# A two-layer hybrid decoder on one core: the last quarter of the first down projection by token with seven block products, and the query projection in another order

## The chip, the cores and the metric

The kernel runs on 1 core of one Trainium2 chip. The metric is the device time of one execution in microseconds. Before the change it is 2163.66 us, the median of 3 runs (2163.54 to 2163.85).

## The reference

One sequence of 256 tokens with 2048 features (float32) goes through two residual layers, each a token mixer and then a ConvFFN, and a last RMSNorm. Only these parts bear on the change:

```python
def rmsnorm(x, g):
    r = lax.rsqrt(jnp.mean(xf * xf, axis=-1, keepdims=True) + EPS)
    return (xf * r).astype(x.dtype) * g

def conv_ffn(xn, w_up, conv_w, conv_b, w_down):
    h = xn @ w_up                                  # 2048 -> 2 * 5632
    ...                                            # causal depthwise conv of width 3
    return (jax.nn.silu(gate) * val) @ w_down      # 5632 -> 2048

def reference(...):
    ...
    h = h + conv_ffn(rmsnorm(h, f_norm[0]), ...)            # first layer's FFN
    k_sh, v_sh, c_sh = fox_shared_kv(h, kv_norm, ...)       # reads rmsnorm(h, kv_norm)
    ...
    q, g = split(rmsnorm(h, b_norm[0]) @ w_qg)              # second layer: queries and gates
    q = rmsnorm(q.reshape(B, S, N_HEADS, HEAD_DIM), q_norm)
    ...
```

So the place in question is the seam between the layers: the first FFN's down projection (5632 to 2048 features) is added to the residual `h`, and the next matrix product, the queries (2048 to 2048 features), needs all 2048 features of the new `h`.

## The kernel before

**Precision.** Each float32 product is made of three TensorE (PE) products of rounded parts: every operand is split into a rounded part (`hi`) and the remainder (`lo`), and hi·hi, hi·lo and lo·hi are summed in PSUM. ScalarE (ACT) makes `hi` by a copy, VectorE (DVE) makes `lo` by a subtraction.

**The weight stream.** All weights come in chunks of 128 x 1024 floats (512 KB), one after the other, in one list (`Stream`). For each item of the list the loop in `run` issues, in this order, the load of the item 6 places on (a DMA in SP's queue into a tile `raw`), the split of the item 3 places on (ACT writes `whi`, DVE writes `wlo`), the matrix products of the item itself on PE, and then one step of every background generator (`advance`). A generator's `yield` therefore means: one chunk later. All engines run their own instructions in this written order. There are 4 buffers each of `raw`, `whi` and `wlo`, so the split of one chunk must wait until PE has done the chunk four places before it:

```python
if 0 <= i + LOADS < n:
    self._load(i + LOADS)
if 0 <= i + AHEAD < n:
    self._split(i + AHEAD)
...
    mult(*self.parts.pop(i))
    self.advance()
```

**Two forms of product.** By features (`feat_block`): the weights are the stationary operand, the result has features on partitions like `h`. By token (`tok_blocks`): the activations are stationary, the weights move, and the result has tokens on partitions, 512 output features a block, 8 chunks a block for 2048 input features. A whole chunk is 24 products of 256 columns in either form. After `between()` the next products are made with 512 columns each, 8 in the first chunk and 2 in the second (`state["wide"]`).

**Seven block products.** In the down projections a chunk by token can be taken as a 2 x 2 block product with seven block multiplications in place of eight (`seven_block`, `seven`): 21 products of 256 columns in place of 24, in two list items of 9 and 12. For that, sums of activation blocks are kept in the operand tile `X1`, which the up projection no longer needs, and sums of the weight blocks are made by DVE for each such chunk (`weight_sums`). A block's seven-product chunks leave sums in a second PSUM tile `m`, which are put together with the plain sums in a tile `Y` at the end of the block (`sums_apart`). `order_of` gives the order of plain and seven-product chunks in a block of 22.

**The seam before the change.** The first down projection has three blocks of 512 columns by token (2, 9 and 9 seven-product chunks). Their results have tokens on partitions and are turned by a DVE transpose of 32 x 32 blocks and a round trip through DRAM (`rows_out`, `rows_in`), then added to `h` (`rows_added`). The last 512 columns are two blocks by features (p = 6 and 7, 11 chunks each), whose results are added to `h` directly; while they run, `residual_prepared` makes the operand `X1` of the queries from the first 12 of 16 feature tiles of `h`. `residual` for p = 6 and 7 makes the last four, and starts the norm: `token_sums` sums the squares over the features with two small products on PE, makes the factor `rcol` of each token, and `token_rows` writes it to DRAM and reads it back as a row (`way_rb`, `rB`), on POOL's queue, for the gates later.

The query projection is four blocks by token, 8 chunks each, one block after the other. When a block is done, `head_norm` normalises its four heads in four steps: squares on ACT and two sums on DVE; twelve small DVE instructions for a reciprocal square root; and twice a scaling and a transpose on DVE, followed by a round trip through DRAM on SP's queue. Beside it `kv_operand` makes the operand `X2` of keys and values from `h`, one tile a step at most.

PSUM holds three tiles `ps` of two banks (`main_ps`) and two tiles `mp` of one bank (`misc_ps`).

Of the kernel before, what the change touches and what calls it, by code (L numbers as in the profile page):

```python
# [17 lines left out]
P = 128  # L18
# [115 lines left out]

class Phase:
# [28 lines left out]
def order_of(blk, lead=3):  # L164


    some, head, foot = {0: (SUMMED[:2], 18, 1), 3: (SUMMED[:6], lead, 5)}.get(blk, (SUMMED, lead, 0))
    plain, seven = [c for c in range(KF // 2) if c not in some], list(some)
    out, rest = [(c, False) for c in plain[:head]], [(c, False) for c in plain[len(plain) - foot:]]
    plain = plain[head:len(plain) - foot]  # L170
    n, m = len(plain), len(seven)
    for i, c in enumerate(plain):
        while len(seven) * n > (n - i - 1) * m and seven:
            out.append((seven.pop(0), True))
        out.append((c, False))
    return out + rest


def build(ctx, tc, d, out):
# [86 lines left out]
    def tok_blocks(blocks, x, K=KD, load=None, prep=None, place=None):  # L266
# [8 lines left out]
        for c, j0, nj in cuts:  # L275
            if prep and c == 3:
                s.then(at_mult=between)
            for i, ((src, done), box) in enumerate(zip(blocks, boxes)):
                def mult(hi, lo, c=c, j0=j0, nj=nj, done=done, box=box):
# [241 lines left out]
    def seven_block(blk, src, order, done, sums_done):  # L521
# [14 lines left out]
        def new_ps():  # L536
            if blk < 3:
                ps = main_ps()
                return lambda tb, w, n=T: ps[:, tb, w:w + n]
# [3 lines left out]
        def products(hi, lo, c, i, j, tb, cols=(0, T), left=0):  # L543
            for lower, part in ((0, hi), (0, lo), (1, hi)):
                n, left = 512 if left > 0 else 256, left - 1
                for w in cols[::n // 256]:
                    mm(box["ps"](tb, w, n), x()[:, 2 * c + j, lower * T + tb * P:lower * T + (tb + 1) * P],
                       part[:, j * 512 + w:j * 512 + w + n],
                       i == 0 and j == 0 and (w == 0 or blk == 3 and tb == 1) and part is hi and not lower,
# [3 lines left out]
        def plain(c, i):  # L553
            def mult(hi, lo):
                if i == 0:
                    box["ps"] = new_ps()
                if blk == 3 and i == 13:
                    s.start(three_blocks())
                if blk < 3 or i <= last - HELD:
# [69 lines left out]
    def sums_apart(blk):  # L629
# [4 lines left out]
        def sums(m):  # L634
            Y = ph.temp("apart", [P, 4, T], bufs=1)
# [7 lines left out]

        def done(ps):
            while "Y" not in box:
# [12 lines left out]
    def rows_added(blk, tb, way, place):  # L658
        for _ in range(3):
# [3 lines left out]
        for _ in range(5):  # L663
# [5 lines left out]
    def residual_prepared():  # L669

        for p in range(6):
            while state["added"] < 2 * (p // 2 + 1):
                yield
            for kt in (2 * p, 2 * p + 1):
                prep(X1, kt, C_BNORM)
                yield
# [8 lines left out]
        state["prepared"] = True  # L685
# [290 lines left out]
    def kv_operand():  # L976
        assert state["prepared"]
        att("X2")
        nc.vector.tensor_tensor(att("gain"), column(C_QNORM), column(C_KNORM), op=OP.mult)
        for _ in range(3):  # L980
            yield
        for kt in range(KD):
            prep(att("X2"), kt, C_KVNORM)
            for _ in range(1 + kt % 2):
                yield
# [40 lines left out]
    def head_norm(key, blk):  # L1026

        def done(*parts):
            parts = [(p, 4 // len(parts) * i) for i, p in enumerate(parts)]
# [211 lines left out]
    def g_done(p):  # L1241
        def done(ps, both):
# [4 lines left out]
            while state["done"] < 2 * p + 2 or state["gates"] < p:  # L1247
# [10 lines left out]
             "prepared": False, "wide": [8, 2]}  # L1258
# [51 lines left out]
    for blk in range(4):  # L1310
        seven_block(blk, d["down1"][22 * blk:22 * blk + 22], order_of(blk), final(blk) if blk < 3 else closing,
                    sums_into_residual(blk))
# [71 lines left out]
```

## Time and profile before

| | |
|---|---|
| Median of 3 runs | 2163.66 us |
| The profiled execution | 2163.74 us, its span 2162.0 us, granted PE clock 0.999 |
| Busy in the span | PE 2152.6, DVE 1649.4, ACT 1212.8, POOL 25.9 us |
| Third down block (by token, seven products) | 869.50 to 926.20 us |
| Two blocks by features | 926.28 to 986.23 us |
| Four query blocks | 986.23 to 1074.01 us |

Times in the rows are from the start of the span. PE is the matrix engine, PEld its weight loads, DVE VectorE, ACT ScalarE, POOL GpSimd, SP the engine that issues most DMAs; SPq is its queue. In a timeline row stand the start, the duration, the engine and line, the operation, `written<-read` tiles and the shape; in square brackets how long the engine had been idle before it, and what ended that. In the profile lines of the kernel before, line 216 is every matrix product, lines 112 and 113 the split of a plain chunk, 313 and 314 an operand tile from `h` (`X` or `att_X`, the program's `X1` and `X2`), 345 and 348 the factor's way through DRAM, 1037 to 1048 `head_norm`.

### The profile page before, as it was taken

What the parts mean: (1) busy time and instruction counts of PE and PEld (TensorE: products, weight loads), DVE (VectorE), ACT (ScalarE), POOL (GpSimd) and SP (SyncE); (2) the same over time, 40 slices, a digit from 0 to 9 for tenths busy, and PEclk for the clock granted to TensorE, in tenths of its full rate; (3) what the DMA queues carried; (4) which work ended last, traced back from release to release, by engine and by line L of the source; (5) the groups of instructions that cost most, each with busy time, mean ns of one, the idle gap of its engine ahead of it and who ended that gap; (6) DMA issues with size and microseconds to landing.
All of it is one profiled execution on the core that took longest, in us unless ns stands there. A gap on an engine that the chain in (4) does not pass through costs nothing.

```text
span 2162.0 us, 45349 instructions
## 1 busy us (share of the span) xinstructions
PE 2152.6 (100%) x18572; PEld 2136.3 (99%) x18572; DVE 1649.4 (76%) x2410; ACT 1212.8 (56%) x1692; POOL 25.9 (1%) x46
## 2 busy tenths in 40 slices
PE   9999999999999999999999999999999999999998
PEld 9999999999999999999999999999999999999998
DVE  6696687776777699976778886668777777779997
ACT  6665555555555555554545775445555555555555
POOL 0000000000000000000000200000000000000000
PEclk9999999999999999999999999999999999999999
DMA  8686566665666567776878877566866666666665
GB/s 311 189 241 205 193 199 194 190 200 184 203 192 194 176 200 228 225 226 179 266 249 260 255 230 234 186 221 197 267 194 195 193 196 192 194 191 188 204 204 166
DMA packets 159857, 454.68 MB, mean 210 GB/s; under 512 B 26320, under 2 KB 48608, under 8 KB 159264
## 3 DMA queue, kind: packets, MB, share of 16 engines
q1 hardware_dynamic: 158112, 447.82, 66.4%
q0 software_dynamic: 1072, 3.41, 0.7%
q8 instruction: 145, 2.38, 0.4%
q10 hardware_dynamic: 464, 0.55, 0.1%
q14 instruction: 64, 0.52, 0.1%
HBM read 434.39 MB, written 17.32 MB: 209 GB/s over the span
## 4 chain that ended last, share of the span: by engine, by line
PE 99%; DVE 0%; ACT 0%; issue 0%; POOL 0%; DVEq 0%; ACTq 0%; POOLq 0%
PE ps L216 98%; PE mp L216 1%; PE mp L780 0%; PE mp L1228 0%; PE ps L1225 0%; ACT sq L441 0%; DVE h_h L747 0%; DVE h_h L440 0%; DVE h_h L741 0%; PE mp L412 0%; ACT fin_t L733 0%; DVE fin_t L737 0%; DVE h_h L717 0%; DVE fin_y L736 0%; DVE rcol L738 0%
## 5 line engine op out<-in xcount | busy, mean ns | idle before, releaser
L113 DVE TENSOR_TENSOR wlo<-raw,whi 128x1024 fp32r<-128x1024 f32 (+1 forms) x732 | 887.3, 1218 | 270.5 <-ACT whi L112 266.3
L112 ACT ACTIVATE whi<-raw 128x1024 fp32r<-128x1024 f32 (+1 forms) x732 | 770.0, 1057 | 570.0 <-PE ps L216 448.5
L216 PE MATMUL ps<-X,whi 128*128 128x256 f32 (+1 forms) x6466 | 823.6, 280 | 0.0
L216 PEld LDWEIGHTS ps<-X,whi 128*128 128x128 f32 x6466 | 775.3, 188 | 6.8
L216 PE MATMUL ps<-X,wlo 128*128 128x256 f32 x3328 | 445.2, 276 | 0.0
L216 PEld LDWEIGHTS ps<-X,wlo 128*128 128x128 f32 x3328 | 409.8, 188 | 1.7
L216 PE MATMUL ps<-whi,ffn_H 128*128 128x256 f32 (+1 forms) x1852 | 303.2, 277 | 0.0
L216 PEld LDWEIGHTS ps<-whi,ffn_H 128*128 128x128 f32 x1852 | 255.4, 188 | 0.7
L216 PE MATMUL ps<-whi,X 128*128 128x256 f32 (+1 forms) x1336 | 221.5, 279 | 0.0
L216 PE MATMUL ps<-wlo,ffn_H 128*128 128x256 f32 (+1 forms) x924 | 192.1, 277 | 0.0
L216 PEld LDWEIGHTS ps<-whi,X 128*128 128x128 f32 x1336 | 187.3, 188 | 1.6 <-ACT whi L112 0.2
L924 DVE SCALAR_TENSOR_TENSOR ffn_room<-ffn_room,col 128x255 f32<-128x255 f32 x352 | 161.8, 481 | 6.4
L216 PE MATMUL ps<-whi,att_X 128*128 128x256 f32 (+2 forms) x970 | 163.8, 285 | 0.0
L216 PEld LDWEIGHTS ps<-wlo,ffn_H 128*128 128x128 f32 x924 | 144.1, 188 | 0.2
L216 PE MATMUL ps<-wlo,X 128*128 128x256 f32 (+1 forms) x666 | 144.3, 279 | 0.0
L392 DVE TENSOR_TENSOR ffn_room<-ps,rB 128x512 f32<-128x512 f32 x76 | 52.5, 691 | 113.2 <-PE ps L216 113.2
L216 PEld LDWEIGHTS ps<-whi,att_X 128*128 128x128 f32 x970 | 135.5, 188 | 3.4
L920 ACT ACTIVATE ffn_room<-ffn_room,col 128x256 f32<-128x256 f32 x176 | 96.3, 595 | 53.5 <-DVE ffn_room L392 53.5
L216 PEld LDWEIGHTS ps<-wlo,X 128*128 128x128 f32 x666 | 106.3, 188 | 0.4
L216 PE MATMUL ps<-wlo,att_X 128*128 128x256 f32 (+2 forms) x476 | 105.7, 286 | 0.0
L90 ACT ACTIVATE whi<-raw 128x768 fp32r<-128x768 f32 x46 | 39.0, 848 | 68.4 <-PE ps L216 50.8
L216 PEld LDWEIGHTS ps<-wlo,att_X 128*128 128x128 f32 x476 | 75.5, 188 | 0.8
(229 smaller groups left out, 1694.5 us busy)
## 6 DMA issues: line engine op xcount, KB each, us to landing
raw<-up SPq DMA_DIRECT2D x352, 512.0 KB, 4.1
raw<-down SPq DMA_DIRECT2D x154, 512.0 KB, 4.3
raw<-a_in_u SPq DMA_DIRECT2D x32, 512.0 KB, 4.4
raw<-a_out SPq DMA_DIRECT2D x32, 512.0 KB, 3.7
raw<-b_q SPq DMA_DIRECT2D x32, 512.0 KB, 4.5
raw<-kvf_v SPq DMA_DIRECT2D x32, 512.0 KB, 5.0
raw<-b_g SPq DMA_DIRECT2D x32, 512.0 KB, 4.1
raw<-b_out SPq DMA_DIRECT2D x32, 512.0 KB, 4.3
```

Source lines behind the costliest of these rows:

```text
L90: self.nc.scalar.activation(hi[:, cols], src[:, cols], AF.Copy)
L112: self.nc.scalar.activation(h, raw, AF.Copy)
L113: self.nc.vector.tensor_tensor(l, raw, h.bitcast(F32), op=OP.subtract)
L216: nc.tensor.matmul(o, a, b, start=start, stop=stop, skip_group_check=True)
L392: nc.vector.tensor_tensor(a, src, rB[:, None, :].to_broadcast([P, 2, T]), op=OP.mult)
L920: nc.scalar.activation(c[:, m, :], a[:, m, :], AF.Identity, scale=w[2], bias=column(C_CONVB + l * 2 * KF + f))
L924: nc.vector.scalar_tensor_tensor(c[:, m, n:], a[:, m, :T - n], w[k], c[:, m, n:], op0=OP.mult, op1=OP.add)
```

## The change

Seven things are altered.

1. The last 512 columns of the first down projection are a fourth block by token, with 8 seven-product chunks, 14 plain ones, four of them at the end (`order_of(blk, 2, (8, 4))`). The two blocks by features are gone, and with them a `between()` ahead of them.
2. `fourth` puts the block's sums together after its last chunk, in a piece of the tile for values, and starts the two round trips; `rows_added` waits 2 and 4 steps there instead of 3 and 5.
3. `residual_prepared` starts when the fourth block's last seven-product chunk is done, since `X1` holds the block sums until then, and makes two operand tiles a step.
4. The squares and their sum are a generator of their own (`residual_squares`), which ends with `token_sums` and `token_rows`.
5. The query projection takes the first 6 chunks (12 operand tiles) of blocks 0, 1 and 2, then the last two chunks of each of these, and then block 3 whole. Block 3 sums in the two `mp` tiles (`Banks`).
6. `kv_operand` waits 8 steps, then makes one tile a step as soon as its part of `h` is there.
7. The weights are laid out for it (`down0` holds all 2048 columns; `down0s` is gone). The second layer keeps its order and its code.

```diff
-def order_of(blk, lead=3):
+def order_of(blk, lead=3, fourth=(6, 5)):
...
-    some, head, foot = {0: (SUMMED[:2], 18, 1), 3: (SUMMED[:6], lead, 5)}.get(blk, (SUMMED, lead, 0))
+    some, head, foot = {0: (SUMMED[:2], 18, 1), 3: (SUMMED[:fourth[0]], lead, fourth[1])}.get(blk, (SUMMED, lead, 0))
...
-                        box["ps"] = main_ps()
+                        box["ps"] = Banks(misc_ps(), misc_ps()) if i == 3 else main_ps()
...
         def sums(m):
+            box["m"] = m
+            if blk == 3:
+                yield from residual_prepared()
+                return
...
+        def fourth(ps):
+            m, Y = box["m"], att("v")[:, 0, :CHUNK].rearrange("p (a b) -> p a b", a=4)
+            nc.scalar.activation(Y[:, 1, :], m[:, 0, :T], AF.Copy)
+            yield
+            nc.vector.tensor_tensor(Y[:, 0, :], Y[:, 1, :], m[:, 0, T:], op=OP.add)
+            nc.vector.tensor_tensor(Y[:, 3, :], Y[:, 0, :], m[:, 1, T:], op=OP.subtract)
+            nc.vector.tensor_tensor(Y[:, 0::2, :], m[:, 1:, :T].to_broadcast([P, 2, T]), Y[:, 0::3, :], op=OP.subtract)
+            Z = [Y[:, 2 * tb:2 * tb + 2, :].rearrange("p a b -> p (a b)") for tb in range(2)]
+            for tb in range(2):
+                nc.vector.tensor_tensor(Z[tb], Z[tb], ps(tb, 0, 512), op=OP.add)
+            for tb in range(2):
+                yield
+                turned = blocks_turned(Z[tb].rearrange("p (h x) -> p h x", h=4))
+                yield
+                s.start(rows_added(blk, tb, rows_out(f"d{blk}{tb}", turned), Z[tb]))
...
-        for _ in range(3):
+        out_for, in_for = (2, 4) if blk == 3 else (3, 5)
+        for _ in range(out_for):
             yield
...
-        for _ in range(5):
+        for _ in range(in_for):
             yield
...
-        for p in range(6):
+        for p in range(8):
             while state["added"] < 2 * (p // 2 + 1):
                 yield
             for kt in (2 * p, 2 * p + 1):
                 prep(X1, kt, C_BNORM)
+            if p == 5:
+                s.start(residual_squares())
+            yield
+
+    def residual_squares():
+
+        for p in range(8):
+            while state["added"] < 2 * (p // 2 + 1):
                 yield
             sq = small.tile([P, 2, T], F32, name="sq", tag="sq", bufs=2)
             nc.scalar.activation(sq, h[:, 2 * p:2 * p + 2, :], AF.Square)
...
-        state["prepared"] = True
+        yield
+        token_sums()
+        state["rows"] = True
+        yield
+        yield from token_rows("b")
...
     def kv_operand():
-        assert state["prepared"]
-        att("X2")
+        for _ in range(8):
+            yield
         nc.vector.tensor_tensor(att("gain"), column(C_QNORM), column(C_KNORM), op=OP.mult)
-        for _ in range(3):
-            yield
         for kt in range(KD):
+            while state["added"] < 2 * (kt // 4 + 1):
+                yield
             prep(att("X2"), kt, C_KVNORM)
-            for _ in range(1 + kt % 2):
-                yield
+            yield
...
-    for blk in range(3):
-        seven_block(blk, d["down0"][22 * blk:22 * blk + 22], order_of(blk, 2), *sums_apart(blk))
-    s.then(at_mult=between)
-    s.then(at_mult=lambda: s.start(residual_prepared()))
-    for p in (6, 7):
-        feat_block(d["down0s"][11 * p - 66:11 * p - 55], ffn_h, KF, residual(p, C_BNORM))
+    for blk in range(4):
+        seven_block(blk, d["down0"][22 * blk:22 * blk + 22], order_of(blk, 2, (8, 4)), *sums_apart(blk))
...
-    for blk in range(4):
-        tok_block(d["b_q"][8 * blk:8 * blk + 8], lambda: X1, head_norm("q", blk))
+    tok_blocks([(d["b_q"][8 * blk:8 * blk + 8], head_norm("q", blk)) for blk in range(4)], lambda: X1,
+               order=[(n, i) for i in range(3) for n in range(6)] + [(n, i) for i in range(3) for n in (6, 7)]
+               + [(n, 3) for n in range(8)])
```

In the rows below the program's instructions stand in their written order on one engine; `ps_`, `whi_` and `wlo_` with a number are one buffer's turn, so one number of `ps_` is one block. PE before, at the end of the second query chunk, with the sum of squares (line 412) and the 512-column products that follow:

```order
L216 MATMUL ps_12222<-wlo_12174,X1_77 128x256 x2
L216 MATMUL ps_12222<-whi_12173,X1_77 128x256 x2
L412 MATMUL mp_12284<-ones_82,acc_78 128x1 x2
L216 MATMUL ps_12222<-whi_12212,X1_77 128x512
L216 MATMUL ps_12222<-wlo_12213,X1_77 128x512
```

PE with the change, at the sum of squares (line 424); `ps_12663` is query block 2, `ps_12222` above query block 0:

```order
L226 MATMUL ps_12663<-whi_12659,X1_77 128x256 x4
L226 MATMUL ps_12663<-wlo_12660,X1_77 128x256 x2
L226 MATMUL ps_12663<-whi_12659,X1_77 128x256 x2
L424 MATMUL mp_12800<-ones_82,acc_78 128x1 x2
L226 MATMUL ps_12663<-whi_12698,X1_77 128x512
L226 MATMUL ps_12663<-wlo_12699,X1_77 128x512
```

The sum of squares has moved from behind the 2nd of the 32 query chunks to behind the 16th: ahead of it stand six chunks each of blocks 0 and 1 and four of block 2.

DVE before, in two of the steps of the first query block's `head_norm` (line 1048 scales, line 953 transposes, 113 splits a chunk, 314 makes a tile of `X2`):

```order
L113 TENSOR_TENSOR wlo<-raw,whi 128x1024
L314 SCALAR_TENSOR_TENSOR att_X_12251<-h_h,col,att_X_12251 128x256
L1048 TENSOR_TENSOR att_big<-ps,att_hr 128x512
L953 STREAM_TRANSPOSE att_turned<-att_big 128x4x4x32
L113 TENSOR_TENSOR wlo<-raw,whi 128x1024 x2
```

DVE with the change, from the third step of block 0's `head_norm` (lines 1096, 1001) into block 1's (lines 1087 to 1091), up to the first of its twelve small instructions:

```order
L113 TENSOR_TENSOR wlo<-raw,whi 128x1024
L326 SCALAR_TENSOR_TENSOR att_X_12556<-h_h,col,att_X_12556 128x256
L1096 TENSOR_TENSOR att_big<-ps,att_hr 128x512
L1001 STREAM_TRANSPOSE att_turned<-att_big 128x4x4x32
L1087 TENSOR_REDUCE att_hv<-sq 128x4 x2
L113 TENSOR_TENSOR wlo<-raw,whi 128x1024
L326 SCALAR_TENSOR_TENSOR att_X_12556<-h_h,col,att_X_12556 128x256
L1096 TENSOR_TENSOR att_big<-ps,att_hr 128x512
L1001 STREAM_TRANSPOSE att_turned<-att_big 128x4x4x32
L1089 TENSOR_SCALAR att_hv<-att_hv 128x8
```

Blocks 0, 1 and 2 now end two chunks apart, so that two of the three stand in the same steps, between the splits of two chunks.

More of the change, by code (lines that the diff above doesn't have):

```diff
@@ L132, in run, with __init__, __getitem__ @@
             self.advance()
+class Banks:
+    def __init__(self, *banks):
+        self.banks = banks
+    def __getitem__(self, at):
+        return self.banks[at[1]][:, at[2]]
 class Phase:
@@ L264, in tok_block, with tok_blocks @@
         tok_blocks([(src, done)], x, K)
-    def tok_blocks(blocks, x, K=KD, load=None, prep=None, place=None):
+    def tok_blocks(blocks, x, K=KD, load=None, prep=None, place=None, order=None):
         boxes = [{} for _ in blocks]
@@ L274, in tok_blocks, with mult @@
             cuts[:3] = [(c, j, 1) for c in range(3) for j in range(2)]
-        for c, j0, nj in cuts:
-            if prep and c == 3:
+        order = order or [(n, i) for n in range(len(cuts)) for i in range(len(blocks))]
+        for n, i in order:
+            (c, j0, nj), (src, done), box = cuts[n], blocks[i], boxes[i]
+            if prep and c == 3 and i == 0:
                 s.then(at_mult=between)
-            for i, ((src, done), box) in enumerate(zip(blocks, boxes)):
-                def mult(hi, lo, c=c, j0=j0, nj=nj, done=done, box=box):
+            if True:
+                def mult(hi, lo, i=i, c=c, j0=j0, nj=nj, done=done, box=box):
                     kt0 = 2 * c + j0
                     if kt0 == 0:
-                        box["ps"] = main_ps()
+                        box["ps"] = Banks(misc_ps(), misc_ps()) if i == 3 else main_ps()
                     ps, xx, left = box["ps"], x(), wide_next()
@@ L519, in weight_sums, with seven_block @@
         return t
-    def seven_block(blk, src, order, done, sums_done):
+    def seven_block(blk, src, order, done, sums_done, closes=False):
         x = ffn_h
@@ L536, in new_ps @@
         def new_ps():
-            if blk < 3:
+            if not closes:
                 ps = main_ps()
@@ L548, in products @@
                        part[:, j * 512 + w:j * 512 + w + n],
-                       i == 0 and j == 0 and (w == 0 or blk == 3 and tb == 1) and part is hi and not lower,
+                       i == 0 and j == 0 and (w == 0 or closes and tb == 1) and part is hi and not lower,
                        i == last and j == 1 and lower == 1)
@@ L556, in mult @@
                     box["ps"] = new_ps()
-                if blk == 3 and i == 13:
+                if closes and i == 13:
                     s.start(three_blocks())
-                if blk < 3 or i <= last - HELD:
+                if not closes or i <= last - HELD:
                     left = wide_next()
@@ L642, in sums @@
             box["Y"] = Y
+        def fourth(ps):
[13 more added lines that the diff above has]
+                s.start(rows_added(blk, tb, rows_out(f"d{blk}{tb}", turned), Z[tb]))
         def done(ps):
+            if blk == 3:
+                yield from fourth(ps)
+                return
             while "Y" not in box:
@@ L976, in kv_operand @@
     def kv_operand():
-        assert state["prepared"]
-        att("X2")
+        for _ in range(8):
+            yield
         nc.vector.tensor_tensor(att("gain"), column(C_QNORM), column(C_KNORM), op=OP.mult)
-        for _ in range(3):
+        for kt in range(KD):
+            while state["added"] < 2 * (kt // 4 + 1):
+                yield
+            prep(att("X2"), kt, C_KVNORM)
             yield
-        for kt in range(KD):
-            prep(att("X2"), kt, C_KVNORM)
-            for _ in range(1 + kt % 2):
-                yield
         for i in range(8):
@@ L1028, in done @@
         def done(*parts):
+            assert state["rows"]
             parts = [(p, 4 // len(parts) * i) for i, p in enumerate(parts)]
@@ L1257, in build @@
     state = {"normed": False, "layer": 0, "v": 0, "done": 0, "gates": 0, "mixed": 0, "scaled": 0, "summed": 0, "added": 0, "kept": False,
-             "prepared": False, "wide": [8, 2]}
+             "rows": False, "wide": [8, 2]}
     cd = dram.tile([NH, T], F32, name="cd")
@@ L1311, in build @@
         seven_block(blk, d["down1"][22 * blk:22 * blk + 22], order_of(blk), final(blk) if blk < 3 else closing,
-                    sums_into_residual(blk))
+                    sums_into_residual(blk), blk == 3)
     s.run()
@@ L1367 @@
     down0 = np.asarray(f_w_down)[0]
-    arrays["down0"], arrays["down0s"] = tok_chunks(down0[:, :1536]), feat_chunks(down0[:, 1536:])
+    arrays["down0"] = tok_chunks(down0)
     down1 = np.asarray(f_w_down)[1][:, order]
```

## The prediction

> **What bounds the kernel now.** First the page: which engine is busy, and which chain ended last.
>
> ```profile
> PE 2152.6 (100%) x18572; PEld 2136.3 (99%) x18572; DVE 1649.4 (76%) x2410; ACT 1212.8 (56%) x1692; POOL 25.9 (1%) x46
> PE 99%; DVE 0%; ACT 0%; issue 0%; POOL 0%; DVEq 0%; ACTq 0%; POOLq 0%
> ```
>
> PE is busy from end to end and 99% of the last chain is PE. Next the waits of PE over the whole span, which are one:
>
> ```profile
> PE mp L780 <- POOL ident L1269: 1.5, 1, 1.5
> ```
>
> So PE has no stall at the seam before, and the change can win only by fewer products or by products at a better pace; any new wait of PE is lost in full. The busy times by stretch show how much room DVE has: the third down block, the two blocks by features, and eight query chunks with one `head_norm` in them.
>
> ```profile
> 869.50:926.20 56.70, 56.70 (x503) 56.70 (x502) 49.41 (x64) 32.14 (x41) 0.00 (x0) 1.00 0.72 221
> 926.20:986.20 60.00, 60.00 (x521) 59.56 (x520) 43.23 (x58) 31.41 (x42) 0.00 (x0) 1.00 0.70 222
> 1011.40:1033.20 21.80, 21.80 (x194) 21.80 (x194) 18.71 (x34) 12.90 (x19) 0.00 (x0) 1.00 0.83 259
> ```
>
> The columns are the stretch, then busy PE, PEld, DVE (fourth), ACT, POOL, the granted clock (1.00), DMA. DVE has 49.41 of 56.70 in the down block, and 18.71 of 21.80 us in the query chunks although only one of four `head_norm`s runs there.
>
> **Fewer products.** PE's timeline gives the pace, in the form by features, at the start of the queries, and later in the queries.
>
> ```profile
> 980.79 1.98 PE L216 MATMUL ps<-ffn_H,whi 128*128 128x256 f32 x16
> 983.51 1.98 PE L216 MATMUL ps<-ffn_H,whi 128*128 128x256 f32 x16
> ...
> 986.70 0.63 PE L216 MATMUL ps<-whi,X 128*128 128x256 f32 x4
> 987.41 0.64 PE L216 MATMUL ps<-whi,X 128*128 128x256 f32 x4
> ...
> 991.88 0.50 PE L412 MATMUL mp<-ones,acc 128*128 128x1 f32 x4
> 992.25 0.48 PE L216 MATMUL ps<-whi,X 128*128 128x512 f32 x1
> ...
> 1074.01 0.28 PE L216 MATMUL ps<-whi,att_X 128*128 128x256 f32 x1
> ```
>
> A chunk by features takes 983.51 - 980.79 = 2.72 us for 24 products, 0.1133 us each. The two blocks have 22 chunks, 528 products. The fourth block by token has 14 plain chunks of 24 and 8 of 21, 504 products. That is 24 fewer, 24 x 0.1133 = **2.72 us** off PE.
>
> Two smaller things go with the blocks by features. From 986.23 to 991.88, where the form changes back, six products take 987.41 - 986.70 = 0.71 us, 0.0045 us more apiece than 0.1133, and the 512-column products after the sum end that; 48 products are 0.22 us. With the change the form does not change there. And the 512-column products ahead of the blocks by features, ten of them, which I put at 0.1 us from the same difference (some 20 halves at 0.0045 us), are not made. If the slower pace came at the new seam as well and stayed until the sum of squares, 16 chunks x 24 x 0.0045 = 1.7 us would go; I take none, as between the down blocks by token, which is the same form, the windows show 503 products in 56.70 us, 0.113 each. Sum of the gains: **3.04 us**.
>
> **The fourth block's own work.** A seven-product chunk costs DVE more, but 8 with 14 plain ones is one fewer than in the third block, whose DVE had 7.3 us to spare; the ten tiles of `X1` made at the block's end cost 10 x 0.48 = 4.8 us. I take no stall; the bound above is 1 us. The turning of the fourth block (five sums, two transposes, two trips through DRAM) is covered by 18 query chunks, 49 us, since tiles 12 to 15 are first read by chunk 18, and the written order makes them behind chunks 12 and 13. The sum of squares stands behind chunk 15; its last term is made by DVE behind the split of chunk 17. With DVE its usual 4 us ahead of PE it is there in time: nothing, bound above 0.5 us. The fourth block needs no new wait for PSUM: query blocks 1 and 2 begin 6 and 12 chunks after the tiles they take over were read.
>
> **The norms of the query blocks.** This is where I expect the time to go. Blocks 0, 1 and 2 end behind chunks 19, 21 and 23 (counted 0 to 31 as they run), so three `head_norm`s of four steps each fall into steps 19 to 26, two at a time; before, they lay eight chunks apart. DVE's timeline gives the price of each step.
>
> ```profile
> 1012.81 1.27 DVE L1039 TENSOR_REDUCE att_hv<-sq 128x4 f32<-128x512 f32 x2
> 1014.00 1.22 DVE L113 TENSOR_TENSOR wlo<-raw,whi 128x1024 fp32r<-128x1024 f32 x1
> 1015.13 0.16 DVE L1041 TENSOR_SCALAR att_hv<-att_hv 128x8 f32<-128x8 f32 x1
> ...
> 1017.43 1.22 DVE L113 TENSOR_TENSOR wlo<-raw,whi 128x1024 fp32r<-128x1024 f32 x1
> ...
> 1058.52 1.22 DVE L113 TENSOR_TENSOR wlo<-raw,whi 128x1024 fp32r<-128x1024 f32 x1
> 1059.66 0.48 DVE L314 SCALAR_TENSOR_TENSOR att_X<-h_h,col,att_X 128x256 fp32r<-128x256 f32 x1
> 1060.06 0.68 DVE L1048 TENSOR_TENSOR att_big<-ps,att_hr 128x512 f32<-128x512 f32 x1
> 1060.78 0.71 DVE L953 STREAM_TRANSPOSE att_turned<-att_big 128x512 f32<-128x512 f32 x1
> 1061.41 1.18 DVE L113 TENSOR_TENSOR wlo<-raw,whi 128x1024 fp32r<-128x1024 f32 x1
> ```
>
> From start to start: the split of a chunk 1.14 us (1058.52 to 1059.66), a tile of `X2` 0.40, the two reductions 1.19 (1012.81 to 1014.00), the twelve small instructions 2.30 (1015.13 to 1017.43), scaling and transpose 1.35 (1060.06 to 1061.41). Each step from 19 to 23 also has a tile of `X2`. DVE's time per step, from one split to the next:
>
> - step 20: 1.14 + 0.40 + 2.30 = 3.84
> - step 21: 1.14 + 0.40 + 1.35 + 1.19 = 4.08
> - step 22: 1.14 + 0.40 + 1.35 + 2.30 = 5.19
> - step 23: as 21, 4.08
> - step 24: 1.14 + 1.35 + 2.30 = 4.79
> - steps 25 and 26: 1.14 + 1.35 = 2.49 each
>
> PE needs 2.72 us a chunk. Steps 20 to 24 take DVE 21.98 us against 13.60, so it falls back by 8.38 us; from step 25 on it gains again. PE stalls for what exceeds DVE's lead. PE waits for `lo` 0.23 us into a chunk, after two products, so that much is free.
>
> How large is the lead? The last row of PE above starts chunk 32, so chunk n starts at 1074.01 - (32 - n) x 2.72: chunk 7 at 1006.01, chunk 9 at 1011.45.
>
> ```profile
> 999.14 1.23 DVE L113 TENSOR_TENSOR wlo<-raw,whi 128x1024 fp32r<-128x1024 f32 x1 [1.11 <-ACT whi L112]
> 1009.74 1.22 DVE L113 TENSOR_TENSOR wlo<-raw,whi 128x1024 fp32r<-128x1024 f32 x1 [6.66 <-ACT whi L112]
> ```
>
> Chunk 7's remainder was ready at 1000.37, a lead of 5.64 us; that is as far ahead as four buffers let DVE get. Chunk 9's was ready at 1010.96, a lead of only 0.49 us, after DVE and ACT had stood idle. Why, the rows of ACT and POOL say:
>
> ```profile
> 1008.65 1.06 ACT L112 ACTIVATE whi<-raw 128x1024 fp32r<-128x1024 f32 x1 [6.82 <-DMA raw<-b_q]
> ...
> 63.70 0.89 POOL L345 DMA_DIRECT2D way_ra<-rcol  x1 [20.35 <-DVE rcol L331]
> 73.31 0.56 POOL L348 DMA_DIRECT2D rB<-way_ra  x1 [8.73 <-DMA way_ra<-rcol]
> ...
> 995.46 0.72 POOL L345 DMA_DIRECT2D way_rb<-rcol  x1 [921.60 <-DVE rcol L331]
> 1007.70 0.55 POOL L348 DMA_DIRECT2D rB<-way_rb  x1 [11.52 <-DMA way_rb<-rcol]
> ...
> 77.14 1.06 ACT L112 ACTIVATE whi<-raw 128x1024 fp32r<-128x1024 f32 x1 [3.15 <-DMA raw<-a_in_v]
> ```
>
> The chunk's load came late, 13.2 us after `rcol` had been sent to DRAM (995.46 to 1008.65), and the other time that this 1 KB write is made the same is seen: 63.70 to 77.14, 13.4 us. The write itself took 11.5 and 8.7 us. In this program a load in flight beside that write is held until it ends. Before the change it hit chunk 9, seven behind the sum of squares, and nothing was lost, since DVE had one `head_norm` for the next eight chunks. With the change the sum stands behind chunk 15, and seven on from 16 is **chunk 23**, just ahead of the pile of norms. With DVE's lead at 0.49 us there, PE loses 8.38 - 0.49 - 0.23 = **7.66 us**.
>
> [...]
>
> **The sum.** The profiled execution took 2163.74 us, 0.08 more than the median: 2163.74 - 3.04 + 7.66 = 2168.36, and 2168.3 as a median.
>
> **The rivals.** *The load is not late, the norms pile up all the same.* Then the lead at chunk 23 is what a `head_norm` in step 19 leaves: the reductions wait for PE to end chunk 19, and squares, split and remainder follow, as at chunk 35 before: its remainder ends 1077.68 on the trace, 4.48 us ahead of its start at 1082.16.
>
> ```profile
> 1076.45 1.23 DVE L113 TENSOR_TENSOR wlo<-raw,whi 128x1024 fp32r<-128x1024 f32 x1 [0.25 <-ACT whi L112]
> ```
>
> PE loses 8.38 - 4.48 - 0.23 = 3.67 us: 2163.74 - 3.04 + 3.67 = 2164.4. For it: the load might slip past the write by a fraction of a microsecond. Against it: both writes in the trace held one.
>
> *Everything is hidden* (the side that is not slower): the new order of the blocks feeds PE without a stall, 2160.7 us. It decides if DVE can be more than 8.2 us ahead at step 20. Against it: the largest lead is 5.64.
>
> *An earlier load is caught.* If the write holds chunk 22's load as well, DVE does chunk 22's remainder some 2 us too late and has no lead at all for what follows: 2.0 + 8.38 = 10.4 us, 2171.1. The same comes out if PE goes on at the slower pace of 986 us after its stalls: 20 chunks x 24 x 0.0045 = 2.2 us more, 2170.5. For it: the new trips through DRAM crowd SP's queue; against it: loads elsewhere land in 4.5 us.
>
> **How the numbers follow.** Main forecast 0.64, rival one 0.17, all hidden 0.04, an earlier load or slower pace 0.15. The range of 8 in 10 takes in the first two and most of the last: 2164.1 to 2171.0. A measurement of this kernel tells some 0.2% from no change, 4.3 us: slower means over 2168.0, faster under 2159.3. The main forecast lies at 2168.3 with about 1 us of doubt on each side, so 0.6 of it counts as slower and 0.4 as the same; with the last rival, slower is 0.53, the same 0.44, faster 0.03.
>
> **What would show it.** In the profile after: PE products down by about 24 in a span without other loss; PE rows with gaps at query chunks 24 to 28, none before; a wait of ACT for `raw` from `b_q` just ahead, about 13 us after `way_rb` is sent; DVE without idle time from there to chunk 29. If PE waits there for less than 3 us, my step prices or the lead are wrong; if the wait is 3 to 4 us, the write did not hold the load; if PE waits in the fourth block or at the sum of squares, I have missed a term.

## The result, and the profile after

The changed kernel takes 2180.79 us (median of 6 runs, 2178.86 to 2188.44), the kernel before 2163.85 us in the same comparison (2163.54 to 2164.42): 1.0082 times as long, with a 95% interval of 1.0067 to 1.0097. It is slower, as forecast, but by 17 us where 4.6 were predicted. The profiled execution took 2182.55 us, 1.8 above the median.

The page of the changed kernel, its busy times, its last chain by engine, and then PE's waits (us in total, times, the longest):

```profile
PE 2164.5 (99%) x18558; PEld 2147.3 (98%) x18558; DVE 1670.0 (77%) x2448; ACT 1222.4 (56%) x1709; POOL 26.1 (1%) x46
PE 96%; DMA 2%; DVE 1%; ACT 0%; issue 0%; SPq 0%; POOL 0%; DVEq 0%; ACTq 0%; POOLq 0%
PE mp L226 <- DVE wlo L113: 4.5, 3, 2.1
PE mp L1140 <- ACT att_f L1135: 1.8, 1, 1.8
PE ps L226 <- DVE wlo L113: 0.7, 1, 0.7
```

PE makes 14 products fewer than before (the 24 fewer that were worked out, less ten, as each of the ten products of 512 columns that went had stood for two) and is busy 11.9 us longer (2164.5 against 2152.6). So only a part of the loss is waiting; most of it lies in products that take longer. Where, the starts of the stages say (the first product that reads `X`, the first that reads `att_X`, the transposes of the forget gates, and the end of the span):

| stage | before | after | difference |
|---|---|---|---|
| up to the queries | 986.23 | 983.28 | -2.95 |
| the four query blocks | 87.78 | 95.07 | +7.29 |
| from there to the forget gates' transposes | 25.55 | 29.17 | +3.62 |
| from there to the end | 1062.48 | 1073.31 | +10.83 |

The first two rows are the prediction: a gain of 3.04 (of which 0.22 belongs to the second row) and a loss of 7.66. The last two, 14.5 us, are not in it.

**The query blocks** went as worked out. First ACT and POOL in the changed kernel, then the split of each chunk on DVE from the late one on:

```profile
1029.76 0.72 POOL L357 DMA_DIRECT2D way_rb<-rcol  x1 [956.04 <-DVE rcol L343]
1039.88 0.56 POOL L360 DMA_DIRECT2D rB<-way_rb  x1 [9.40 <-DMA way_rb<-rcol]
1043.40 1.06 ACT L112 ACTIVATE whi<-raw 128x1024 fp32r<-128x1024 f32 x1 [3.70 <-DMA raw<-b_q]
...
1044.50 1.22 DVE L113 TENSOR_TENSOR wlo<-raw,whi 128x1024 fp32r<-128x1024 f32 x1 [4.06 <-ACT whi L112]
1048.33 1.22 DVE L113 TENSOR_TENSOR wlo<-raw,whi 128x1024 fp32r<-128x1024 f32 x1
1052.37 1.21 DVE L113 TENSOR_TENSOR wlo<-raw,whi 128x1024 fp32r<-128x1024 f32 x1
1057.51 1.22 DVE L113 TENSOR_TENSOR wlo<-raw,whi 128x1024 fp32r<-128x1024 f32 x1
1061.56 1.22 DVE L113 TENSOR_TENSOR wlo<-raw,whi 128x1024 fp32r<-128x1024 f32 x1
1066.30 1.22 DVE L113 TENSOR_TENSOR wlo<-raw,whi 128x1024 fp32r<-128x1024 f32 x1
1068.79 1.18 DVE L113 TENSOR_TENSOR wlo<-raw,whi 128x1024 fp32r<-128x1024 f32 x1
```

The load came 13.6 us after the factor had been sent (13.2 and 13.4 before). From split to split DVE then took 3.83, 4.04, 5.14, 4.05, 4.74 and 2.49 us; predicted were 3.84, 4.08, 5.19, 4.08, 4.79 and 2.49. No idle time stands in brackets from 1048 on. PE's waits for `wlo` fell at chunks 25, 26 and 28; at chunk 27 the clock was at half (0.50 from 1060.07 to 1063.48 us) and PE was still at work when the remainder came, which is why the waits add up to 4.5 us only.

**The forget gates.** Behind the queries come `kvf_ks` and `kvf_fk`, and one chunk later PE turns the forget gates, which ACT copies from PSUM. ACT in the changed kernel, and PE:

```profile
1100.49 1.06 ACT L112 ACTIVATE whi<-raw 128x1024 fp32r<-128x1024 f32 x1 [3.19 <-PE ps L226]
1103.77 1.06 ACT L112 ACTIVATE whi<-raw 128x1024 fp32r<-128x1024 f32 x1 [2.22 <-DMA raw<-kvf_k]
1104.74 0.71 ACT L1116 ACTIVATE att_q<-att_rows,att_gain 128x512 f32<-128x512 f32 x1
1105.64 1.06 ACT L112 ACTIVATE whi<-raw 128x1024 fp32r<-128x1024 f32 x1 [0.20 <-DMA raw<-kvf_k]
1106.60 0.70 ACT L1116 ACTIVATE att_q<-att_rows,att_gain 128x512 f32<-128x512 f32 x1
1107.21 0.42 ACT L1135 ACTIVATE att_f<-ps,rcol 128x16 f32<-128x16 f32 x2
...
1107.52 0.44 PE L1140 MATMUL mp<-ident,att_f 128*16 128x128 f32 x2 [1.81 <-ACT att_f L1135]
1108.18 0.63 PE L226 MATMUL ps<-wlo,att_X 128*128 128x512 f32 x1
1108.61 1.05 PE L226 MATMUL ps<-whi,att_X 128*128 128x512 f32 x2
```

ACT's copy stands in its order behind splits of key chunks whose loads are late, and PE waits for it. In the kernel before the same copy was made just in time, a seam without any slack, which I had not looked at; ACT and PE there:

```profile
1099.01 0.42 ACT L1087 ACTIVATE att_f<-ps,rcol 128x16 f32<-128x16 f32 x2
...
1099.55 0.38 PE L1092 MATMUL mp<-ident,att_f 128*16 128x128 f32 x2
```

Behind the wait the products of 512 columns start 0.43 us apart (1108.18 to 1108.61) where 0.23 is usual (1100.01 to 1100.24 in the kernel before): the granted clock was 0.50 from 1107.86 to 1111.27 us.

**The rest.** The same stretches in the two kernels, first 20 us in the key blocks and then 60 us in the output projection, before and after (columns as in the prediction):

```profile
1113.00:1133.00 20.00, 20.00 (x179) 20.00 (x179) 17.15 (x37) 8.61 (x10) 0.00 (x0) 1.00 0.79 256
1370.00:1430.00 60.00, 60.00 (x532) 60.00 (x531) 40.36 (x50) 30.71 (x40) 0.00 (x0) 1.00 0.58 186
```

```profile
1113.00:1133.00 20.00, 20.00 (x171) 20.00 (x170) 16.73 (x30) 10.23 (x12) 0.00 (x0) 1.00 0.75 242
1370.00:1430.00 60.00, 60.00 (x510) 60.00 (x509) 36.91 (x44) 27.45 (x35) 0.00 (x0) 1.00 0.58 188
```

PE is busy throughout at the full clock, and yet makes 171 products where it made 179, and 510 where it made 532 (a stretch also counts the one or two that reach into it). By their starts they are 118.7 and 118.3 ns apart in place of 113.3. All long rows of products that read `X2` (`att_X`) are so (118.3 to 120.0), and those of the gates between them, which read `X`, are not (113.3 to 113.6). That is where most of the last row of the table went, and no view of waits shows any of it.

### The profile page after: what moved, and what is told of

It reads as the page before. It is cut to its first block, busy times and chain, and to the rows that moved or that the text cites. A ratio compares the mean times of both kernels' runs of the same rounds, so it can differ in the third digit from the quotient of the medians.

```text
span 2180.8 us, 45399 instructions
## 1 busy us (share of the span) xinstructions
PE 2164.5 (99%) x18558; PEld 2147.3 (98%) x18558; DVE 1670.0 (77%) x2448; ACT 1222.4 (56%) x1709; POOL 26.1 (1%) x46
## 3 DMA queue, kind: packets, MB, share of 16 engines
q0 software_dynamic: 1072, 3.41, 0.7%
## 4 chain that ended last, share of the span: by engine, by line
PE 96%; DMA 2%; DVE 1%; ACT 0%; issue 0%; SPq 0%; POOL 0%; DVEq 0%; ACTq 0%; POOLq 0%
PE ps L226 94%; PE mp L226 1%; DMA raw<-b_q 1%; DVE wlo L113 0%; DMA raw<-kvf_k 0%; ACT whi L112 0%; DMA att_rows<-way_q 0%; DMA kept<-h_h 0%; DMA raw<-kvf_ks 0%; PE mp L828 0%; DVE att_big L1096 0%; PE mp L1276 0%; PE ps L1273 0%; DMA raw<-kvf_fk 0%; DVE att_hv L1087 0%
## 5 line engine op out<-in xcount | busy, mean ns | idle before, releaser
L113 DVE TENSOR_TENSOR wlo<-raw,whi 128x1024 fp32r<-128x1024 f32 (+1 forms) x724 | 877.3, 1217 | 271.7 <-ACT whi L112 267.4
L112 ACT ACTIVATE whi<-raw 128x1024 fp32r<-128x1024 f32 (+1 forms) x724 | 761.7, 1057 | 563.3 <-PE ps L226 442.0
L226 PE MATMUL ps<-whi,ffn_H 128*128 128x256 f32 (+1 forms) x2124 | 347.1, 277 | 0.0
L226 PEld LDWEIGHTS ps<-whi,ffn_H 128*128 128x128 f32 x2124 | 292.8, 188 | 0.7
L226 PE MATMUL ps<-wlo,ffn_H 128*128 128x256 f32 (+1 forms) x1060 | 220.6, 277 | 0.0
L226 PE MATMUL ps<-whi,X 128*128 128x256 f32 (+1 forms) x1272 | 213.7, 279 | 0.0
L226 PEld LDWEIGHTS ps<-whi,X 128*128 128x128 f32 x1272 | 180.4, 188 | 1.4
L226 PEld LDWEIGHTS ps<-wlo,ffn_H 128*128 128x128 f32 x1060 | 165.6, 188 | 0.2
L90 ACT ACTIVATE whi<-raw 128x768 fp32r<-128x768 f32 x54 | 45.8, 848 | 79.4 <-PE ps L226 58.6
L90 ACT ACTIVATE whi<-ffn_room 128x512 fp32r<-128x512 f32 x108 | 64.2, 627 | 30.5 <-PE ps L226 18.7
```

The lines of the kernel that those rows point to most:

```text
L90: self.nc.scalar.activation(hi[:, cols], src[:, cols], AF.Copy)
L112: self.nc.scalar.activation(h, raw, AF.Copy)
L113: self.nc.vector.tensor_tensor(l, raw, h.bitcast(F32), op=OP.subtract)
L226: nc.tensor.matmul(o, a, b, start=start, stop=stop, skip_group_check=True)
```

## The experiments

Times are medians; the kernel before gave 2163.4 to 2163.9 us in each comparison. The stages in the text are those of the table above, from each run's trace.

**1. Is it the place of `X2`?** In the changed kernel `fourth` asks for the tile of values first, so `X2` no longer begins at byte 99168 of each partition but at 119680. One kernel moves it on by 32 bytes, another moves it in the kernel before.

```diff
+        if key == "X2":
+            ph.keep("ahead", [P, 8])
```

> The changed kernel with one thing altered: the operand tile X2 stands 32 bytes further on in every partition (byte 119712, as X1, H and the weight tiles a multiple of 32 but not of 64; in the changed kernel it came to byte 119680, a multiple of 64, because the tile of values is now asked for first; before the change 99168). Theory 'place': products that read X2 take 118.7 ns at 119680 and 113.3 ns at 99168 or 119712; their excess over 113.3 in the trace of the changed kernel adds up to about 12 us (0.9 at 1078 to 1101, 7.5 from 1111 to 1279, 3.7 from 1370 to 1464), so 2180.8 - 12 = 2169 us. Theory 'state': the stalls around 1050 to 1107 and the half clock there leave PE at a slower pace which the 512-column products no longer end; then 32 bytes change nothing, 2180.8 us.

> The kernel before with one thing altered: X2 stands 32 bytes further on (byte 99200, a multiple of 64, in place of 99168). No stall, no other order. Theory 'place': its X2 products go from 113.3 to 118.7 ns, some 2200 of them, 2163.7 + 12 = 2175.5 us. Theory 'state': no stall, so no slower pace, 2163.7 us.

Measured: 2180.7 us, and 2173.2 us (1.0046, interval 1.0031 to 1.0061). So 32 bytes alone cost the kernel before 9.3 us, without a stall and with the old order. Its row in the output projection:

```profile
1370.00:1430.00 60.00, 60.00 (x510) 60.00 (x509) 36.97 (x45) 28.33 (x36) 0.00 (x0) 1.00 0.56 185
```

The place matters, but a multiple of 64 is not what decides, as 119712 was as bad as 119680. Four more kernels put `X2` at other places. The first, shown here, asks for `X2` ahead of the values again; the other three are the changed kernel with 120, 24 and 56 floats put ahead of `X2` in place of the 8 above:

```diff
+            att("X2")
             m, Y = box["m"], att("v")[:, 0, :CHUNK].rearrange("p (a b) -> p a b", a=4)
```

> The changed kernel, but the tile X2 is asked for ahead of the tile of values, so that X2 is at byte 99168 again, as before the change, and nothing else is altered. Moving X2 32 bytes on in the kernel before cost 9.3 us (2173.2 against 2163.9) and no stall was in it, so the place matters; but 119712 was no better than 119680, so a multiple of 64 is not what decides. If the old place is a good one whatever the order of the work: X2 products back at 113.3 ns and 9.3 us less than the changed kernel, 2171.5 us; what is left over the predicted 2168.3 is then the stall at the forget gates (1101 to 1111 in the trace of the changed kernel). If the slower pace has a second cause in the new order: no gain, 2180.8 us.

> The changed kernel with X2 at byte 120160 (96 above a multiple of 128, 352 above a multiple of 512, as X1 at 7520 and H and X2 at 99168, which all ran at 113.3 ns; the slow places were 0 and 32 above a multiple of 128, 384 and 416 above one of 512). If the remainder of the address decides, X2 products take 113.3 ns and the time is as e6_x2_first; if the upper part of the address does (above 119 thousand), 118.7 ns and about 2181 us.

> The changed kernel with X2 at byte 119776 (96 above a multiple of 128, but 480 above one of 512). If the remainder to 128 decides, as e6_x2_first; if that to 512 does, 118.7 ns and about 2181 us.

> The changed kernel with X2 at byte 119904: 96 above a multiple of 256, as the good places 99168 and 120160, but 96 above one of 512, where these are 352. If the remainder to 256 decides: X2 products at 113.3 ns, about 2171.6 us as e6_x2_first. If that to 512 does: 117 to 119 ns, 2177 to 2181 us.

Measured: 2171.62 us with the old place (1.0034, interval 1.0021 to 1.0047), 9.2 us less than the changed kernel; 2171.7, 2177.4 and 2170.7 us for the other three, of one run each. Among these places the remainder to 256 tells the good from the bad:

| byte of `X2` | remainder to 256 | products in 20 us, key blocks | products in 60 us, output |
|---|---|---|---|
| 99168 (before) | 96 | 179 | 532 |
| 120160 | 96 | 179 | 532 |
| 119904 | 96 | 179 | 531 |
| 119680 (after) | 128 | 171 | 510 |
| 99200 | 128 | 170 | 510 |
| 119712 | 160 | 171 | 502 |
| 119776 | 224 | 172 | 512 |

**2. Its own place, or its distance from the weights?**

```diff
     col = const.tile([P, C_ALL], F32, name="col")
     const.tile([P, 16], F32, name="spare")
...
+    const.tile([P, 8], F32, name="ahead")
     wpool = ctx.enter_context(tc.tile_pool(name="wpool", bufs=AHEAD + 1))
```

That is one kernel, the kernel before with 32 bytes put ahead of its tiles; the other leaves `X2` and moves the weight parts that are multiplied with it:

```diff
-            s.chunk(src[c], mult, TOK_AT)
+            s.chunk(src[c], mult, 40)
```

> The kernel before with 32 bytes put ahead of nearly all of its tiles: X1, H, X2 and the weight tiles all move by 32 bytes together. If the distance between the two operands of a product decides (by token the weights stand 192 above the operand tile to a multiple of 256, by features the operand tile 192 above the weights, in the kernel before): no change, 2163.7 us. If the place of each tile by itself decides: nearly all 18,500 products take some 5 ns longer, 90 us more.

> The changed kernel, X2 left at byte 119680, but the weight parts that are multiplied with X2 stand 32 bytes further on in their tiles (by token from column 40 in place of 32, by features from 8 in place of 0), which gives the distance of 192 to a multiple of 256 that the kernel before has. If the distance decides: X2 products at 113.3 ns and 9.2 us less than the changed kernel, 2171.6 us. If the place of X2 by itself does: 2180.8 us.

Measured: 2163.8 us (one run) with everything moved together, `X2` to the byte 99200 that was bad alone, so its own place is not what counts; and 2173.24 us (1.0046, interval 1.0030 to 1.0063) with the weights moved, 7.5 of the 9.2 us. The key blocks and the output projection of this second kernel:

```profile
1113.00:1133.00 20.00, 20.00 (x179) 20.00 (x178) 17.80 (x36) 9.85 (x11) 0.00 (x0) 1.00 0.79 250
1370.00:1430.00 60.00, 60.00 (x512) 60.00 (x511) 37.10 (x46) 28.36 (x36) 0.00 (x0) 1.00 0.56 185
```

The key blocks make 179 products in 20 us again, with `X2` at the bad place. **By token the distance between the two operands decides.** By features, in the output projection, this kernel still makes 512 in 60 us where the kernel before makes 532, although the distance is the good one there as well. The slower pace of the 48 products at 986 us in the kernel before, 117.8 ns, also came with a change of operands and stayed until the next 512-column products, of which there are none ahead of the output projection; whether that is the reason here was not tried.

**3. Does the factor's write hold the load?** A first kernel (on `X2` at 119712) only moved the write 30 steps on in the written order.

> As e1_x2_place, and the factor's write to DRAM (way_rb) is sent 30 steps later, behind the query blocks. Theory of the prediction (the write holds the load of chunk 23 and takes DVE's lead just ahead of the pile of norms): 4 us less than e1_x2_place. Rival (the lead at chunk 23 does not come from that write, or the norms' own trips on SP's queue set the stall): the same as e1_x2_place within 1 us.

Measured: 2182.0 us. It tells nothing of the load: POOL sent the write at 1029.82 us all the same, as it has nothing else to do and waits for `rcol` alone. The second kernel gives POOL something later to wait for:

```diff
+            src = ph.keep("rcol2", [P, 128])[:, :2]
+            nc.vector.tensor_copy(src, rcol)
-        nc.gpsimd.dma_start(way.rearrange("o (t p) -> p (o t)", t=2), rcol)
+        nc.gpsimd.dma_start(way.rearrange("o (t p) -> p (o t)", t=2), src)
```

> As e6_x2_first, and the factor's write to DRAM (way_rb) is made from a copy of rcol that DVE makes 30 steps later, so that POOL cannot send it before the query blocks have ended (in e3_late_write POOL, which waits for nothing but rcol, sent it at 1029.82 us all the same, as it runs ahead of the written order). Theory of the prediction: no load is held at chunk 23, DVE keeps a lead of about 4.5 us, the query blocks lose 3.7 instead of 7.4 us: 4 us less than e6_x2_first in the query blocks. Rival: the lead at chunk 23 is lost anyway, no change there.

Measured: the query blocks take 91.25 us against 94.50 in `e6_x2_first`, a loss of 3.5 against 6.7 over the 87.78 of before; predicted were 3.7 and 7.7 for the load on time and late. But the whole is 2173.2 us, 1.6 us more. POOL, ACT and PE of this kernel:

```profile
1118.41 0.72 POOL L360 DMA_DIRECT2D way_rb<-att_rcol  x1 [1044.90 <-DMA way_k<-att_turned]
1128.78 0.55 POOL L363 DMA_DIRECT2D rB<-way_rb  x1 [9.65 <-DMA way_rb<-att_rcol]
1130.27 1.06 ACT L112 ACTIVATE whi<-raw 128x1024 fp32r<-128x1024 f32 x1 [8.29 <-DMA raw<-kvf_k]
1140.13 0.50 PE L226 MATMUL ps<-wlo,att_X 128*128 128x256 f32 x2 [1.08 <-DVE wlo L113]
```

The load beside the write was late where it now went: its chunk was split 11.9 us after the write was sent (1118.41 to 1130.27), and PE waited four times from 1131 to 1140 (the last in the row above). The cost had moved, and the stretch to the forget gates took 29.72 us in place of 27.83 on top.

**4. Is it the pile of norms?** The blocks' ends are spread, and the tiles of `X2` begin 4 steps earlier; first with `X2` at a bad place (119712), then at the good one. The two alterations were not tried apart.

```diff
-               order=[(n, i) for i in range(3) for n in range(6)] + [(n, i) for i in range(3) for n in (6, 7)]
-               + [(n, 3) for n in range(8)])
+               order=[(n, i) for i in range(3) for n in range(6)] + [(n, i) for a in range(3) for n, i in
+               ((6, a), (7, a), (2 * a, 3), (2 * a + 1, 3))] + [(6, 3), (7, 3)])
```

> As e1_x2_place, and the blocks' ends are spread: behind the first 18 chunks the last two of block 0, two of block 3, the last two of block 1, two of block 3, the last two of block 2, four of block 3, so that the norms begin behind chunks 19, 23, 27 and 31; and the tiles of X2 begin 4 steps earlier. The factor's write stays where it was. Theory of the prediction (DVE's pile of norms stalls PE for 7.4 us in the query blocks): DVE then has 10.75 us of work for every 10.88 us of PE and nothing more than 1 us is lost: about 7 us less than e1_x2_place, 2161 to 2162 us. Rival (the trips through DRAM on SP's queue, which stay as many, set the stalls): no more than 2 us less than e1_x2_place.

> e6_x2_first and the spread of the blocks' ends of e4_spread (norms behind chunks 19, 23, 27 and 31, X2 four steps earlier). In e4_spread the query blocks lost nothing, where they lost 6 to 7 us without it, and yet the whole was only 4.4 us shorter, because PE then waited 3.4 us at the forget gates and ran some us there at half clock. Theory 'taken back': the loads of the first key chunks come at a time of their own, and the forget gates wait for them: again only some 4 us less than e6_x2_first, 2167.5 us, with 3 us or more lost at the forget gates. Rival: the stall there came from the bad place of X2 (products 5 ns longer, clock), then all 7 us are gained, 2164.5 us.

Measured: 2176.3 us and 2164.69 us (1.0003, interval 0.9994 to 1.0013). In both the query blocks take 87.6 us, as before the change: the pile of norms and `X2` tiles was the whole of their loss. The first gained only 4.4 us over `e1_x2_place` where 7 were expected, as the stretch to the forget gates grew from 28.03 to 29.89 us and the rest by 1.6. In the second the whole is 6.9 us shorter than `e6_x2_first`, nearer to the rival of that expectation. But the stall at the forget gates did not go with the bad place, as that rival had it: the stretch there takes 29.66 us, 4.1 more than before the change, which is about what the whole lies above 2160.7, and it holds the longest wait of PE in this kernel:

```profile
PE mp L1141 <- ACT att_f L1136: 2.7, 1, 2.7
PE mp L829 <- POOL ident L1318: 1.5, 1, 1.5
PE ps L226 <- DVE wlo L113: 0.8, 1, 0.8
```

**5. What makes the forget gates late?** On `e6_x2_first`, PE's transposes one step later, or the eight writes of `h` to DRAM (`kept`) 20 steps later; then both on the spread order.

```diff
+        yield
         yield
         between()
```

```diff
+        for _ in range(20):
+            yield
         for i in range(8):
```

> e6_x2_first, and only PE's two transposes of the forget gates one step later. If ACT's copy of the gates is late by 2.2 us only because of the key chunks' splits ahead of it in ACT's order: one chunk (2.7 us) covers it and the 2.3 us lost there are gained, 2169.3 us. If the splits themselves are late as well, PE waits for wlo one chunk on, and nothing is gained.

> e6_x2_first, and only the eight writes of h to DRAM (kept, 256 KB each) 20 steps later. If these writes, which stand between the loads in SP's queue from 1066 to 1103 us, make the loads of the key chunks late: the stall at the forget gates goes, 2.3 us less than e6_x2_first. If the query norms' writes (way_q) do, which wait for DVE in the same queue: no change.

> e10_spread_first, and two things more: PE's two transposes of the forget gates one step (one chunk) later, and the eight writes of h to DRAM (kept) 20 steps later, so that they don't stand in SP's queue among the loads of the first key chunks. If the stall at the forget gates is what is left: 2163.5 - 3.0 = 2160.5 us, the sum of the prediction without any stall. If a wait for the loads of the key chunks takes its place (PE then waits for wlo in the key chunks instead): no less than 2164 us.

Measured: the transposes alone 2170.46 us (2168.84 to 2172.24), within the spread of `e6_x2_first` (2169.95 to 2172.68). The wait of 2.0 us at the transposes is gone, but PE then waits for `wlo` twice, 0.8 us in all. The writes alone 2168.73 us (2167.55 to 2176.27), 2.9 us less in the median, and the stretch to the forget gates 26.39 us in place of 27.83: by the trace these writes, 256 KB for every two chunks in SP's queue, are part of what makes the loads late; the times by themselves overlap. All together **2160.69 us** (2159.45 to 2163.52, 10 runs), 0.9986 times the kernel before, interval 0.9976 to 0.9995. PE's waits in that kernel are the one that the kernel before has:

```profile
PE mp L829 <- POOL ident L1321: 1.5, 1, 1.5
```

This version is 3.0 us faster than the kernel before (interval 1.1 to 5.2), which is the sum without stalls, 2163.74 - 3.04 = 2160.7, and 20 us faster than the changed kernel.

## Why the prediction was right and wrong

- **Fewer products, the fourth block, the sum of squares: right.** The queries begin 2.95 us earlier where 2.82 were worked out (3.04 without the 0.22 of the query stage), and no wait of PE lies in the fourth block. That it comes so close is in part luck: in the other kernels with the same first part they begin at 982.42 to 983.93 us (983.28 here). The rows beside the pace of 0.0045 us give 0.0050 (0.71 by 6, less 0.1133); over all 48 products it is 0.0045. The final kernel came out at the sum without stalls.
- **The pile of norms: right, step by step.** Six DVE steps agreed to 0.05 us, the late load to 0.4 us, the loss in the query blocks was 7.29 where 7.66 less 0.22 were worked out. The spread of the blocks took it away, and the late write took 3.25 of the 4.0 us that the held load was said to cost. The half clock, which I had not thought of, came in the query blocks too, and by luck cost nothing there: PE had to wait for DVE at the next chunk all the same.
- **"Sum 2163.74 - 3.04 + 7.66": wrong, since it ended at the last query chunk.** It took all behind chunk 32 as unchanged. Two terms were missing, 9.2 and some 2.3 us of the 12.5 by which the median was missed. About 1 us is not placed; it is within what the second term differs between kernels of the same order.
- **The place of `X2`, 9.2 us** (`e6_x2_first` against the changed kernel; 9.3 the other way round). I read `att("v")` in `fourth` only as a piece of memory to put sums in. But who asks first decides where each tile lies, and the code had two signs of it: `PAD`, `FEAT_AT` and `TOK_AT`, which set the weights at another column for each form, and two tiles that nothing writes or reads, `spare` (line 189) and `place` (line 200). A tile without a use is there for where it puts the others.
- **The forget gates, about 2.3 us** (the stretch to the transposes: 27.83 in `e6_x2_first`, 25.55 before; in `e7_x2_mod512` and `e15_x2_mod256`, with the same order and `X2` at a good place, 28.76 and 29.19, which would be 3.2 and 3.6). The prediction said that DVE "gains again" from step 25 on. DVE does, but the loads do not: in SP's queue they stand behind the norms' writes, which wait for DVE (twice, 1.4 us in all, from 1060 to 1108 us), and behind `kept`, and the next seam that had no slack got the delay. Of these only `kept` was tried alone; the share of the norms' writes is argued from the order of the queue.
- **The rivals.** "PE goes on at the slower pace after its stalls" named the right sign with the wrong cause and a quarter of the size; such a pace does follow a stall at times (18 products at 117.8 ns behind a wait of 1.08 us in `e9_late_write`), but it is not what the changed kernel lost by. "The load is not late" was put at 3.67 us and measured at 3.5 when made so. The range was too narrow: but for 2.2 us of a slower pace, both its ends took in the query blocks alone.

## What to carry to other kernels

When an edit makes a new tile or asks for an old one earlier, list where every operand of TensorE lies before and after, not only what is computed when; and read tiles that have no use as a warning. Follow a stall past its stage: name the next place whose result comes just in time, since the delay is handed on there, in the loads' queue too. And look at what an instruction waits for before moving it in the written order: 30 steps did not move the write of `e3_late_write`, which POOL sent at 1029.82 us all the same.

## What the runs showed of the hardware

- **Products of 256 columns with a weight load each went at 113.3 ns, or at 117 to 120, and the place of their two operands to each other is one cause** (`e16_all_moved`, where both moved: 179 in 20 us as before; `e17_weights_moved`, where the weights did: 179 by token in place of 171). The weight parts begin at byte 42912 of a partition (160 above a multiple of 256) by features and 128 bytes further on by token. In the kernel before, the moving operand of every such product of the weight stream lies 192 bytes above the stationary one, to a multiple of 256. In the changed kernel it is 160 by token and 224 by features for the products that read `X2`, and their long rows went at 118.7 to 120.0 and at 118.3 ns. At 128 and 0 (`e1_x2_place`) 171 were made in 20 us by token and 502 in 60 us by features, at 64 in both forms (`e8_x2_mod128`) 172 and 512, where the kernel before made 179 and 532; other distances were not tried. It is 9.2 us here, with PE shown as busy at the full clock.
- **A pace of 117.8 ns also comes at the good distance, and its cause is open.** It was seen in 48 products behind the change of form at 986 us and in 24 from 1096.73 us on in the kernel before, in 22 from 1049.83 us on in the changed kernel, and in 18 behind a wait of 1.08 us in `e9_late_write` (1140.47 to 1142.59 us). In the output projection of `e17_weights_moved` 512 were made in 60 us.
- **Half clock, twice before the end of the changed kernel, each time behind 3.41 us in which PE was busy for less than half.** The two falls, each with the stretch ahead of it (columns as before; the granted clock is the third from the end):

```profile
1056.66:1060.07 3.41, 1.28 (x11) 1.28 (x12) 3.24 (x9) 1.06 (x1) 0.00 (x0) 1.00 0.43 93
1060.07:1063.48 3.41, 3.41 (x19) 3.41 (x18) 3.38 (x6) 0.67 (x1) 0.00 (x0) 0.50 0.86 290
1104.44:1107.86 3.42, 1.61 (x14) 1.33 (x14) 2.36 (x2) 3.23 (x7) 0.00 (x0) 1.00 0.98 390
1107.86:1111.27 3.41, 3.41 (x10) 2.65 (x10) 2.67 (x5) 3.12 (x6) 0.00 (x0) 0.50 0.84 294
```

  Both spells at half clock last 3.41 us, and the second begins 47.79 us after the first, 14 times that length. No single wait of PE was over 2.2 us. In the stretches of the same length beside these (1049.84 to 1056.66, 1063.48 to 1070.31 and 1101.04 to 1104.44 us) PE was busy for 2.65 to 3.01 us each, and the granted clock behind them was 1.00. The length of a wait alone does not tell whether half clock follows: it did behind 1.8 us at the forget gates of the changed kernel, and behind 2.7 us at those of `e10_spread_first` PE went on at full pace (products of 512 columns 0.23 us apart, 1101.68 to 1101.91 us).
- **A 1 KB write from POOL's queue** took 8.7 to 11.5 us at each of the four places where it was seen (8.73 and 11.52 in the kernel before, 9.40 with the change, 9.65 in `e9_late_write`), and the chunk whose load was beside it was split 11.9 to 13.6 us after the write was sent (13.4, 13.2, 13.6 and 11.9).
